# Weights of an encoder step laid out on the host in the order of the kernel's loads

## The chip, the cores and the metric

The kernel runs on one core of a Trainium2 chip. The metric is device time in microseconds (us) of one execution. The engines are PE (TensorE, matmuls), DVE (VectorE), ACT (ScalarE), POOL (GpSimd) and SP (SyncE, which here issues every transfer); 16 DMA engines move data between HBM and the on-chip memory. A float32 product is made of float32r parts: a value is split into a high and a low part, and three matmuls (high x high, high x low, low x high) are added up.

## The reference

One layer of a streaming encoder is computed for 2048 prompt tokens and 32 sample tokens, in blocks of 512, 512, 512 and 544 tokens:

```python
def split_proj(a, w_in):
    z = a @ w_in
    qa, ka, va, qb, kb, vb = jnp.split(
        z, [WIDTH_A, 2 * WIDTH_A, 3 * WIDTH_A, 3 * WIDTH_A + WIDTH_B, 3 * WIDTH_A + 2 * WIDTH_B], axis=-1)
...
def merge(oa, ob, subln_g, out_norm_b, w_out, lam_init):
    oa = rmsnorm(oa, subln_g, SUBLN_EPS) * (1.0 - lam_init)
    ob = rmsnorm(ob.reshape(B, T, WIDTH_B), out_norm_b)
    return jnp.concatenate([oa.reshape(B, T, WIDTH_A), ob], axis=-1) @ w_out
...
def ffn_ple(h, p, g_mlp, w_up, w_down, w_ple_gate, w_ple_proj):
    c = rmsnorm(h, g_mlp)
    h = h + jnp.square(jax.nn.relu(c @ w_up)) @ w_down
    return h + jax.nn.sigmoid(h @ w_ple_gate) * (p @ w_ple_proj)
```

Between split_proj and merge stand a differential attention over all earlier tokens (group A, four heads of two maps) and a band attention over the last 576 tokens (group B, eight heads). The model width is 1024; w_in has 3072 columns, w_up 4096, w_down 4096 rows, w_ple_proj 256 rows.

## The kernel before, in words

The work runs in stages. First the rows of x are normalized and turned (prep), and w_in makes v (vtile, 256 columns at a time) and q and k (proj, 128 columns at a time); attention of groups A and B is woven between. q, k, v, attention outputs (oT) and the residual (hS) go through scratch buffers in HBM, so transfers of weights share the DMA engines with these. From about 800 us follow the output projection (outproj), the MLP and the gate (gate) by token block: blocks 0 and 1 with an ordinary MLP (mlp_up, mlp_down), blocks 2 and 3 from about 2200 us with mlp7, which makes the up-projection out of seven products of half-sized parts in place of eight.

Every weight comes in units of 512 KB: a raw tile "wr" of 4 KB in each of 128 partitions is loaded by SP, then split into high and low parts: ACT writes the high part, POOL (in a few places DVE) the low one. Function wunit does that, for all weights but those of mlp7's up-projection; the tiles are wh and wl, or, late in the kernel, "piece" tiles of half the size, which turn round in rings of buffers. There are two raw buffers, three or four in some stages; SP issues a load once the last reader of its buffer is done. A unit of w_in (q, k), w_up, w_out or w_ple_gate is the 1024 rows of 128 columns, in each partition eight rows of 512 bytes; a unit for v is 512 rows of 256 columns, four pieces of 1 KB; a unit of w_down or w_ple_proj is 256 rows of 512 columns, two pieces of 2 KB.

In mlp7 a chunk of 256 columns of w_up comes as two loads of 512 rows each. Its function weights (L1239 on) makes the parts a11, a21 (first load) and a12, a22 (second load), and with DVE the sums a11 - a21 (L1255), s2 = a22 minus that (L1256), s1 (L1257) and s4 (L1258). The sums overwrite the raw tiles. The first chunk of a block goes into a tile "lead".

The order of the instructions on every engine is made by a scheduler ahead of the run; it simulates the program with its own estimate of each instruction and transfer. Engines work through their rows in order, so a row that waits holds up all rows behind it.

Of the kernel before, what the change touches and what calls it, by code (L numbers as in the profile page):

```python
# [13 lines left out]
F32 = mybir.dt.float32  # L14
# [6 lines left out]
P = 128  # L21
# [122 lines left out]
class Kern:  # L144
# [266 lines left out]
        return [(0, 512 * b, 512), (512, SP + PAST, SS)]  # L411

    def vunits(self, grp, c, **kw):
        col = 1536 * grp + 1024 + 256 * c
        wv = self.a["w_in"][0][:, col : col + 256].rearrange("(k p) c -> p k c", p=P)
        return [self.wunit(wv[:, 4 * i : 4 * i + 4], [4, 256], **kw) for i in range(2)]

    def vtile(self, b, i, grp, c, u, acts, sg, mm):
        nc, a = self.nc, self.a
# [29 lines left out]

    def proj(self, half, grp, acts, sg, mm, tp, vs=range(2), gs=range(4)):  # L450
        nc, a = self.nc, self.a
        W = a["w_in"][0]
        base = 1536 * grp
        ko_p, ko_s = (a["ka_p"], a["ka_s"]) if grp == 0 else (a["kb_p"], a["kb_s"])
        for c in vs:
            u = self.vunits(grp, c)
            for b in half:
                for i in range(len(toks(b))):
                    self.vtile(b, i, grp, c, u, acts, sg, mm)
                    yield  # L460
        late = []
        for g in gs:
            gi = 4 * grp + g
            for kind in range(2):
                col = base + 512 * kind + P * g
                wh, wl = self.wunit(W[:, col : col + P].rearrange("(k p) c -> p k c", p=P), [8, P])
                for b in half:
                    aH, aL = acts[b]
                    hi = sg.tile([P, BLK], F32R, tag="qh", bufs=2, name="qh")
                    lo = sg.tile([P, BLK], F32R, tag="ql", bufs=2, name="ql")  # L470
                    if kind == 1:
                        raw = sg.tile([P, BLK], F32, tag="kr", bufs=2, name="kr")
                    for s0, n in SUBS[b]:
                        ps = mm.tile([P, 512], F32, tag="mm", name="qps")
                        self.mm3(
                            ps[:, :n],
                            [
                                (wh[:, k], wl[:, k], aH[:, k, s0 : s0 + n], aL[:, k, s0 : s0 + n])
                                for k in range(8)
                            ],  # L480
                        )
# [12 lines left out]
                        self.split(h_, l_, r_, "act", "pool")  # L494
                    if kind == 0:
                        for i, t in enumerate((hi, lo)):
                            self.dma(
                                self.qS[gi, :, :, 2 * b : 2 * b + 2, i].rearrange("m r k c -> (m r) k c"),
                                t[:, :512].rearrange("p (k c) -> p k c", c=256),
                            )  # L500
                            if b == 3:
                                self.dma(
                                    self.qS[gi, :, :, 8, i, :SS].rearrange("m r c -> (m r) c"), t[:, 512 : 512 + SS]
                                )
                        yield
                        continue
                    for i, t in enumerate((hi, lo)):
                        for c0, kc, n in self.ktok(b):
                            self.dma(self.kS[gi, i, :, kc : kc + n], t[:, c0 : c0 + n])
                    yield  # L510

                    def knat(b=b, g=g, raw=raw):
                        if grp == 0 or b == 3:
                            tps = tp.tile([P, 4, P], F32, tag="mm", name="ktp")
                            for i in range(4):
                                nc.tensor.transpose(tps[:, i], raw[:, i * P : i * P + P], self.ident)
                            kn = sg.tile([P, 4, P], F32, tag="kn", bufs=2, name="kn")
# [439 lines left out]
    def outproj(self, b, wk, oact, ps, acc):  # L957
        nc, a = self.nc, self.a
        n, t0 = BN[b], 512 * b
        W = a["w_out"][0]  # L960
        sq = wk.tile([P, BLK], F32, tag="acc", bufs=2, name="sqacc2")[:, :n]
        acc.append(sq)
        for d in range(8):
            wh, wl = self.wunit(W[:, P * d : P * d + P].rearrange("(k p) c -> p k c", p=P), [8, P])
# [145 lines left out]

    def mlp_up(self, ch, nf, blocks, st, wk, up, mm):
        nc = self.nc
        Wu = self.a["w_up"][0]
        us, w = {}, {}
        order = [(f, b) for f in range(nf) for b in blocks]
        if ch == 0:
# [1 line left out]
        for f, b in order:  # L1118
            ft = nf * ch + f
            if f not in w:  # L1120
                w[f] = self.wunit(Wu[:, P * ft : P * ft + P].rearrange("(k p) c -> p k c", p=P), [8, P])
            wh, wl = w[f]
            h, cH, cL = st[b]
            uh = up.tile([P, up.aw], F32R, tag="u", name="uh")
# [13 lines left out]

    def mlp_down(self, ch, nf, blocks, us, st, wk, mm):
        nc = self.nc  # L1140
        Wd = self.a["w_down"][0]
        nd = 8 // nf
        for dh in range(nf):
            wh, wl = self.wunit(
                Wd[P * nf * ch : P * nf * (ch + 1), P * nd * dh : P * nd * (dh + 1)].rearrange(
                    "(f p) c -> p f c", p=P
                ),
                [nf, P * nd],
            )
            for d in range(nd):  # L1150
                dd = nd * dh + d
                for b in blocks:
# [36 lines left out]
    def mlp7(self, b, hh, box, ops, wk, up, mm, md):  # L1189
        nc = self.nc  # L1190
        n = BN[b]
        m = n // 2
        Wu, Wd = self.a["w_up"][0], self.a["w_down"][0]

        def downs(ch, us):
            for dh in range(2):
                wh, wl = self.wunit(
                    Wd[2 * P * ch : 2 * P * (ch + 1), 512 * dh : 512 * dh + 512].rearrange("(f p) c -> p f c", p=P),
                    [2, 512],
                )  # L1200
# [38 lines left out]
        def weights(ch, w, piece):  # L1239
            raws = []  # L1240
            for i in range(2):
                raws.append(self.rawp.tile([P, 4, 256], F32, bufs=2, name="wr"))
                self.dma(
                    raws[i],
                    Wu[512 * i : 512 * i + 512, 256 * ch : 256 * ch + 256].rearrange("(k p) c -> p k c", p=P),
                )
            a11, a21 = raws[0][:, :, :P], raws[0][:, :, P:]
            a12, a22 = raws[1][:, :, :P], raws[1][:, :, P:]
            names = ("a11", "a12", "s2", "s1")
            for x in names:  # L1250
                w[x] = piece([4, P])
# [71 lines left out]
    def gate(self, b, h, up, act, md, wk=None, made=None):  # L1323
        nc, a = self.nc, self.a
        n, t0 = BN[b], 512 * b
        Wg, Wp = a["w_ple_gate"][0], a["w_ple_proj"][0]
        pT = [[up.tile([P, BLK], F32R, tag="u", name="pT") for _ in range(2)] for _ in range(2)]
        for i in range(2):
            for k in range(2):
# [13 lines left out]
            for k in range(8):  # L1343
                self.split(hH[k], hL[k], h[:, k, :n], "act", "dve" if k % 2 else "pool")
        for dq in range(2):
            ph, pl = self.wunit(
                Wp[:, 512 * dq : 512 * dq + 512].rearrange("(k p) c -> p k c", p=P), [2, 512]
            )
            for d4 in range(4):
                d = 4 * dq + d4  # L1350
                wh, wl = self.wunit(Wg[:, P * d : P * d + P].rearrange("(k p) c -> p k c", p=P), [8, P])
# [335 lines left out]
}  # L1687


# [26 lines left out]
```

## Time and profile before

| | |
|---|---|
| runs before | 3106.78, 3105.26, 3100.71 us; median 3105.26 us |
| the profiled execution | 3106.68 us, of which 3104.9 us are the span from the first to the last instruction |
| mean granted TensorE clock | 0.988 |
| PE busy | 2990.2 us, 96% of the span |
| DVE, ACT, POOL busy | 59%, 57%, 60% |
| transfers | 523,279 packets, 539.19 MB, 174 GB/s over the span |
| weight loads | 402 of 512 KB: w_up 128, w_down 128, w_in 74, w_out 32, w_ple_gate 32, w_ple_proj 8 |

The profile is of one execution. Its rows of waits name an engine, a tile and a line, what that engine waited for, and then the total in us, how often, and the longest. A row of the timeline has the start, the duration in us and what the instruction does (written tile <- read tiles); in brackets stands the idle time just before and what ended it. The slices are 40 equal parts of the span, each digit the busy share in tenths. A row of stages has the stretch, its length, the busy time and instructions of PE, PE's weight loads, DVE, ACT and POOL, the granted clock, the busy share of the DMA engines and GB/s.

### The profile page before, as it was taken

Reading aid. Unit: us, or ns where it says so; the run is one execution under the profiler, and the core shown is the slowest. Engines: PE = TensorE matmul, PEld = TensorE weight load, DVE = VectorE, ACT = ScalarE, POOL = GpSimd, SP = SyncE. Lnnn points to the kernel's source line nnn. Section 1 sums busy time; section 2 is a strip of 40 time slices with the busy share of each in tenths; the row PEclk is TensorE's granted clock in tenths of the full one; section 3 lists DMA queues with packets and bytes.
Section 4 is the critical chain, followed back from the end, with each engine's and each line's share of the span. In section 5 each row is a group of like instructions: output and inputs, shape, how many; then the busy total and the mean of one; then the engine's idle time right before and its main releaser. Section 6 shows DMA issues by size and latency. Waiting matters only on the chain. (4 is left out here: it accounts for less than half of the span.)

```text
span 3104.9 us, 51763 instructions
## 1 busy us (share of the span) xinstructions
PE 2990.2 (96%) x17801; PEld 2637.0 (85%) x17801; DVE 1826.0 (59%) x4404; ACT 1776.4 (57%) x3434; POOL 1852.7 (60%) x2512
## 2 busy tenths in 40 slices
PE   8999989999899999999999999999899999999998
PEld 7788879899777888878888888878788887999998
DVE  6157565564565455456666656635667885576663
ACT  6256565765666666556556556554655555554545
POOL 2456746413446544556655555677878888767674
PEclk9999999999999999999999999999999999999999
DMA  9798776976877554555655454348434446333231
GB/s 283 258 263 247 224 218 187 280 221 186 247 230 226 159 155 136 154 157 167 196 152 140 124 145 139 123 150 260 155 116 130 146 158 226 118 109 102 90 117 57
DMA packets 523279, 539.19 MB, mean 174 GB/s; under 512 B 38749, under 2 KB 401569, under 8 KB 523017
## 3 DMA queue, kind: packets, MB, share of 16 engines
q1 hardware_dynamic: 523016, 535.89, 57.5%
q8 instruction: 141, 2.31, 0.3%
q14 instruction: 122, 0.99, 0.1%
HBM read 421.97 MB, written 117.75 MB: 174 GB/s over the span
## 5 line engine op out<-in xcount | busy, mean ns | idle before, releaser
L176 POOL TENSOR_TENSOR wl<-wr,wh 128x256 fp32r<-128x256 f32 x648 | 478.9, 771 | 317.8 <-ACT wh L181 277.9
L181 ACT ACTIVATE piece<-wr 128x512 fp32r<-128x512 f32 x406 | 245.4, 624 | 265.0 <-PE ups L217 111.2
L176 POOL TENSOR_TENSOR piece<-wr,piece 128x256 fp32r<-128x256 f32 x404 | 327.5, 836 | 104.6 <-ACT piece L181 85.7
L181 ACT ACTIVATE wh<-wr 128x1024 fp32r<-128x1024 f32 x228 | 240.4, 1055 | 188.1 <-PE ups L217 46.8
L166 POOL TENSOR_TENSOR wl<-wr,wh 128x256 fp32r<-128x256 f32 x264 | 201.9, 797 | 188.1 <-ACT wh L181 185.3
L216 PE MATMUL dps<-uh,piece 128*128 128x272 f32 (+1 forms) x768 | 246.3, 324 | 6.2 <-DVE h L1217 2.5
L166 POOL TENSOR_TENSOR piece<-wr,piece 128x256 fp32r<-128x256 f32 x280 | 235.1, 871 | 26.7 <-ACT piece L181 25.5
L218 PE MATMUL dps<-uh,piece 128*128 128x272 f32 (+1 forms) x768 | 246.9, 324 | 1.8 <-POOL piece L166 1.6
L217 PE MATMUL dps<-ul,piece 128*128 128x272 f32 (+1 forms) x768 | 247.3, 323 | 0.2 <-DVE ul L187 0.2
L216 PE MATMUL ups<-cs,piece 128*128 128x256 f32 (+1 forms) x864 | 245.8, 285 | 0.9 <-DVE r L1228 0.8
L217 PE MATMUL ups<-cs,piece 128*128 128x256 f32 (+1 forms) x864 | 245.7, 285 | 0.0
L218 PE MATMUL ups<-cs,piece 128*128 128x256 f32 (+1 forms) x864 | 245.5, 284 | 0.0
L216 PE MATMUL qps<-aH,wh 128*128 128x512 f32 (+1 forms) x640 | 227.9, 357 | 1.1 <-DVE ql L488 1.1
L217 PE MATMUL qps<-aL,wh 128*128 128x512 f32 (+1 forms) x640 | 228.0, 356 | 0.0
L218 PE MATMUL qps<-aH,wl 128*128 128x512 f32 (+1 forms) x640 | 227.6, 356 | 0.0
L1217 DVE TENSOR_TENSOR h<-h,dps 128x272 f32<-128x272 f32 (+1 forms) x384 | 188.9, 514 | 52.6 <-PE dps L218 51.7
L1169 DVE TENSOR_TENSOR h<-h,dps 128x512 f32<-128x512 f32 x256 | 173.3, 682 | 69.0 <-PE dps L218 67.4
L665 ACT ACTIVATE e<-e,nm 128x128 f32<-128x128 f32 (+16 forms) x136 | 157.2, 1156 | 94.9 <-DVE nm L663 92.9
L216 PE MATMUL dps<-uh,wh 128*128 128x512 f32 x512 | 207.0, 404 | 1.8 <-DVE h L1169 1.8
L216 PE MATMUL ups<-cH,wh 128*128 128x512 f32 x512 | 202.8, 397 | 1.9 <-ACT cH L181 1.9
L217 PE MATMUL ups<-cL,wh 128*128 128x512 f32 x512 | 202.5, 396 | 1.8 <-POOL cL L166 1.2
L218 PE MATMUL ups<-cH,wl 128*128 128x512 f32 x512 | 202.7, 396 | 0.0
(311 smaller groups left out, 9369.8 us busy)
## 6 DMA issues: line engine op xcount, KB each, us to landing
wr<-w_up SPq DMA_DIRECT2D x128, 512.0 KB, 4.0
wr<-w_down SPq DMA_DIRECT2D x128, 512.0 KB, 3.9
wr<-w_in SPq DMA_DIRECT2D x74, 512.0 KB, 5.5
q<-qS SPq DMA_DIRECT2D x128, 256.0 KB, 5.2
v<-vSa SPq DMA_DIRECT2D x64, 512.0 KB, 4.8
ka<-kS SPq DMA_DIRECT2D x32, 512.0 KB, 6.8
wr<-w_out SPq DMA_DIRECT2D x32, 512.0 KB, 4.6
wr<-w_ple_gate SPq DMA_DIRECT2D x32, 512.0 KB, 4.2
```

The costliest lines, as they stand in the source:

```text
L166: nc.gpsimd.tensor_tensor(out[:, sl], a[:, sl], b[:, sl], op=op)
L176: nc.gpsimd.tensor_tensor(out[:, sl], a[:, sl], b[:, sl], op=op)
L181: nc.scalar.activation(hi, raw, AF.Copy)
L216: nc.tensor.matmul(ps, lh, rh, start=start and i == 0, stop=False)
L217: nc.tensor.matmul(ps, lh, rl, start=False, stop=False)
L218: nc.tensor.matmul(ps, ll, rh, start=False, stop=stop and i == n - 1)
L665: nc.scalar.activation(row, row, AF.Exp, bias=nmx, accum_out=z[:nr, m : m + 1])
L1169: nc.vector.tensor_tensor(hv, hv, ps, op=ALU.add)
L1217: nc.vector.tensor_tensor(hv, hv, ps, op=ALU.add)
```

## The change

On the host, numpy cuts each weight into the units of the loads and lays them one behind the other, so that a unit is 128 rows (partitions) of 4 KB without a gap. w_in becomes two arrays, w_qk and w_v. The function tiled does it, and each load names its unit by a number:

```diff
+def tiled(w, k, c):
+    r = w.shape[0] // (k * P)
+    w = w.reshape(r, k, P, -1, c).transpose(0, 3, 2, 1, 4)
+    return np.ascontiguousarray(w.reshape(-1, P, k, c))
...
+    w_in = arrays.pop("w_in")[0]
+    arrays["w_qk"] = tiled(np.concatenate([w_in[:, :1024], w_in[:, 1536:2560]], 1), 8, P)
+    arrays["w_v"] = tiled(np.concatenate([w_in[:, 1024:1536], w_in[:, 2560:]], 1), 4, 256)
+    for n, k, c in (("w_out", 8, P), ("w_up", 8, P), ("w_down", 2, 512), ("w_ple_gate", 8, P), ("w_ple_proj", 2, 512)):
+        arrays[n] = tiled(arrays[n][0], k, c)
...
-                wh, wl = self.wunit(W[:, col : col + P].rearrange("(k p) c -> p k c", p=P), [8, P])
+                wh, wl = self.wunit(a["w_qk"][8 * grp + 4 * kind + g], [8, P])
...
             raws = []
             for i in range(2):
-                raws.append(self.rawp.tile([P, 4, 256], F32, bufs=2, name="wr"))
-                self.dma(
-                    raws[i],
-                    Wu[512 * i : 512 * i + 512, 256 * ch : 256 * ch + 256].rearrange("(k p) c -> p k c", p=P),
-                )
-            a11, a21 = raws[0][:, :, :P], raws[0][:, :, P:]
-            a12, a22 = raws[1][:, :, :P], raws[1][:, :, P:]
+                raws.append(self.rawp.tile([P, 8, P], F32, bufs=2, name="wr"))
+                self.dma(raws[i], self.a["w_up"][2 * ch + i])
+            a11, a12 = raws[0][:, :4], raws[0][:, 4:]
+            a21, a22 = raws[1][:, :4], raws[1][:, 4:]
```

The other loads are changed like the one of proj. The tiles, their buffers and the splits stay. In mlp7 a load is now all 1024 rows of 128 columns (the unit that mlp_up uses), so the first load holds a11 and a12 and the second a21 and a22.

The scheduler's order is the same on PE, DVE, ACT and POOL up to the gate of block 0, which is woven with the first chunk of mlp7 for block 2. (Line numbers after the change are lower: L1234 to L1237 are the sums that were L1255 to L1258, L1011 was L1017, L1338 to L1343 were L1362 to L1367.) ACT at this gate, before: piece_25153 is the high part of the second half of a gate weight (raw tile wr_25146), cs the parts of the MLP's input made from tmp, sig the gate's activation.

```order
L181 ACTIVATE cs_24507<-tmp_24983 128x256
L1364 ACTIVATE sig_25041<-sig_25041 128x512
L181 ACTIVATE cs_24505<-tmp_24980 128x256
L181 ACTIVATE cs_24499<-tmp_25057 128x256
L181 ACTIVATE cs_24503<-tmp_24980 128x256
L181 ACTIVATE piece_25153<-wr_25146 128x512
L181 ACTIVATE cs_24501<-tmp_25060 128x256
```

ACT at the same place after the change:

```order
L1340 ACTIVATE sig_25041<-sig_25041 128x512
L181 ACTIVATE cs_24507<-tmp_24983 128x256
L181 ACTIVATE cs_24499<-tmp_25057 128x256
L181 ACTIVATE cs_24505<-tmp_24980 128x256
L181 ACTIVATE piece_25153<-wr_25146 128x512
L181 ACTIVATE cs_24501<-tmp_25060 128x256
L181 ACTIVATE cs_24509<-tmp_25060 128x256
L1343 ACTIVATE sig_25041<-sig_25041 128x512
L181 ACTIVATE cs_24503<-tmp_24980 128x256
```

The row cs_24503 has moved from ahead of piece_25153 to behind it. DVE at the same gate, before, from the first sum of mlp7's first chunk on (wr_25200 and wr_25202 are its two raw tiles):

```order
L1255 TENSOR_TENSOR wr_25200<-wr_25200 128x4x128
L1256 TENSOR_TENSOR s2_25210<-wr_25202,wr_25200 128x512
L1366 TENSOR_SCALAR sig_24964<-gps_24939,sig_24964 128x512
L1017 TENSOR_SCALAR tmp_24980<-tmp_24980,g_mlp_s_245,r_24417 128x512
L1257 TENSOR_TENSOR wr_25200<-s2_25210,wr_25200 128x4x128
L187 TENSOR_TENSOR lead_25199<-s2_25210,lead_25199 128x512
L1017 TENSOR_SCALAR tmp_24983<-tmp_24983,g_mlp_s_245,r_24417 128x512
L1381 TENSOR_TENSOR sig_24964<-sig_24964,pps_24970 128x512
L1258 TENSOR_TENSOR wr_25202<-wr_25202,s2_25210 128x4x128
```

DVE there after the change:

```order
L1234 TENSOR_TENSOR wr_25202<-wr_25200,wr_25202 128x512
L1342 TENSOR_SCALAR sig_24964<-gps_24939,sig_24964 128x512
L1011 TENSOR_SCALAR tmp_24980<-tmp_24980,g_mlp_s_245,r_24417 128x512
L1235 TENSOR_TENSOR s2_25210<-wr_25202 128x512
L1011 TENSOR_SCALAR tmp_24983<-tmp_24983,g_mlp_s_245,r_24417 128x512
L1357 TENSOR_TENSOR sig_24964<-sig_24964,pps_24970 128x512
L1236 TENSOR_TENSOR wr_25200<-s2_25210,wr_25200 128x512
L1237 TENSOR_TENSOR wr_25200<-wr_25200,s2_25210 128x512
L187 TENSOR_TENSOR lead_25199<-s2_25210,lead_25199 128x512
```

The first sum reads both raw tiles, and the second only the second one; the second sum has moved behind two rows of the gate and the norm. In the later chunks of mlp7, here in block 3, DVE had before (r0, u2, u3 and r1 are the results of the seven products, h the residual that dps is added to):

```order
L1228 TENSOR_TENSOR u2_30228<-t1_30199,ups_30229 128x272
L1255 TENSOR_TENSOR wr_30624<-wr_30624 128x4x128
L1228 TENSOR_TENSOR u3_30258<-u2_30228,ups_30259 128x272
L1228 TENSOR_TENSOR r0_30197<-u2_30228,ups_30275 128x272
L187 TENSOR_TENSOR piece_30345<-wr_30314,piece_30344 128x512
L1228 TENSOR_TENSOR r1_30198<-u3_30258,ups_30293 128x272
L187 TENSOR_TENSOR ul_30194<-r0_30197,uh_30193 128x544
L1228 TENSOR_TENSOR r0_30357<-t1_30359,ups_30374 128x272
L1228 TENSOR_TENSOR u2_30388<-t1_30359,ups_30389 128x272
L1256 TENSOR_TENSOR s2_30642<-wr_30626,wr_30624 128x512
L1217 TENSOR_TENSOR h_30191<-h_30191,dps_30415 128x272
```

DVE in the same chunk after the change:

```order
L187 TENSOR_TENSOR ul_30194<-r0_30197,uh_30193 128x544
L1210 TENSOR_TENSOR r0_30357<-t1_30359,ups_30374 128x272
L1210 TENSOR_TENSOR u2_30388<-t1_30359,ups_30389 128x272
L1234 TENSOR_TENSOR wr_30626<-wr_30624,wr_30626 128x512
L1235 TENSOR_TENSOR s2_30642<-wr_30626 128x512
L1199 TENSOR_TENSOR h_30191<-h_30191,dps_30415 128x272
```

The first sum has moved down seven rows, to stand just ahead of the second.

More of the change, by code (lines that the diff above doesn't have):

```diff
@@ L413, in vunits @@
     def vunits(self, grp, c, **kw):
-        col = 1536 * grp + 1024 + 256 * c
-        wv = self.a["w_in"][0][:, col : col + 256].rearrange("(k p) c -> p k c", p=P)
-        return [self.wunit(wv[:, 4 * i : 4 * i + 4], [4, 256], **kw) for i in range(2)]
+        return [self.wunit(self.a["w_v"][4 * i + 2 * grp + c], [4, 256], **kw) for i in range(2)]
     def vtile(self, b, i, grp, c, u, acts, sg, mm):
@@ L451, in proj @@
         nc, a = self.nc, self.a
-        W = a["w_in"][0]
-        base = 1536 * grp
         ko_p, ko_s = (a["ka_p"], a["ka_s"]) if grp == 0 else (a["kb_p"], a["kb_s"])
@@ L464, in proj @@
             for kind in range(2):
-                col = base + 512 * kind + P * g
-                wh, wl = self.wunit(W[:, col : col + P].rearrange("(k p) c -> p k c", p=P), [8, P])
+                wh, wl = self.wunit(a["w_qk"][8 * grp + 4 * kind + g], [8, P])
                 for b in half:
@@ L959, in outproj @@
         n, t0 = BN[b], 512 * b
-        W = a["w_out"][0]
         sq = wk.tile([P, BLK], F32, tag="acc", bufs=2, name="sqacc2")[:, :n]
@@ L963, in outproj @@
         for d in range(8):
-            wh, wl = self.wunit(W[:, P * d : P * d + P].rearrange("(k p) c -> p k c", p=P), [8, P])
+            wh, wl = self.wunit(a["w_out"][d], [8, P])
             h = wk.tile([P, BLK], F32, tag="tmp", bufs=self.nt, name="hd")[:, :n]
@@ L1112, in mlp_up @@
         nc = self.nc
-        Wu = self.a["w_up"][0]
         us, w = {}, {}
@@ L1120, in mlp_up @@
             if f not in w:
-                w[f] = self.wunit(Wu[:, P * ft : P * ft + P].rearrange("(k p) c -> p k c", p=P), [8, P])
+                w[f] = self.wunit(self.a["w_up"][ft], [8, P])
             wh, wl = w[f]
@@ L1140, in mlp_down @@
         nc = self.nc
-        Wd = self.a["w_down"][0]
         nd = 8 // nf
         for dh in range(nf):
[L1144 to L1148, printed above, removed]
-            )
+            wh, wl = self.wunit(self.a["w_down"][nf * ch + dh], [nf, P * nd])
             for d in range(nd):
@@ L1192, in mlp7 @@
         m = n // 2
-        Wu, Wd = self.a["w_up"][0], self.a["w_down"][0]
         def downs(ch, us):
             for dh in range(2):
[L1197 to L1200, printed above, removed]
+                wh, wl = self.wunit(self.a["w_down"][2 * ch + dh], [2, 512])
                 for d in range(4):
@@ L1241, in weights @@
             for i in range(2):
-                raws.append(self.rawp.tile([P, 4, 256], F32, bufs=2, name="wr"))
-                self.dma(
-                    raws[i],
-                    Wu[512 * i : 512 * i + 512, 256 * ch : 256 * ch + 256].rearrange("(k p) c -> p k c", p=P),
-                )
-            a11, a21 = raws[0][:, :, :P], raws[0][:, :, P:]
-            a12, a22 = raws[1][:, :, :P], raws[1][:, :, P:]
+                raws.append(self.rawp.tile([P, 8, P], F32, bufs=2, name="wr"))
+                self.dma(raws[i], self.a["w_up"][2 * ch + i])
+            a11, a12 = raws[0][:, :4], raws[0][:, 4:]
+            a21, a22 = raws[1][:, :4], raws[1][:, 4:]
             names = ("a11", "a12", "s2", "s1")
@@ L1325, in gate @@
         n, t0 = BN[b], 512 * b
-        Wg, Wp = a["w_ple_gate"][0], a["w_ple_proj"][0]
         pT = [[up.tile([P, BLK], F32R, tag="u", name="pT") for _ in range(2)] for _ in range(2)]
@@ L1345, in gate @@
         for dq in range(2):
-            ph, pl = self.wunit(
-                Wp[:, 512 * dq : 512 * dq + 512].rearrange("(k p) c -> p k c", p=P), [2, 512]
-            )
+            ph, pl = self.wunit(a["w_ple_proj"][dq], [2, 512])
             for d4 in range(4):
                 d = 4 * dq + d4
-                wh, wl = self.wunit(Wg[:, P * d : P * d + P].rearrange("(k p) c -> p k c", p=P), [8, P])
+                wh, wl = self.wunit(a["w_ple_gate"][d], [8, P])
                 for s0, sn in SUBS[b]:
```

## The prediction

> **What bounds the kernel now.** I read the page from the top (span, busy times, slices), then the waits of the tensor engine, and behind its longest ones the waits of the engine that it waits for, in the same 20 us.
>
> ```profile
> span 3104.9 us, 51763 instructions
> PE 2990.2 (96%) x17801; PEld 2637.0 (85%) x17801; DVE 1826.0 (59%) x4404; ACT 1776.4 (57%) x3434; POOL 1852.7 (60%) x2512
> DMA  9798776976877554555655454348434446333231
> core 0: 3104.9 us, clock 0.988
> ```
>
> PE is the bound: it is idle for 3104.9 - 2990.2 = 114.7 us in all, and its mean granted clock of 0.988 costs about 0.012 x 3105 = 37 us more. No change to weight loads can bring more than these together. The DMA row says where loads are scarce: the first ten slices (0 to 780 us) are 60 to 90% busy, the last five 10 to 30%. What ends the idle time of PE, in the whole run:
>
> ```profile
> PE css L1096 <- ACT sh L181: 5.9, 1, 5.9
> PE gps L216 <- ACT piece L181: 5.2, 2, 5.0
> PE xp L380 <- DMA x<-x_prompt: 4.4, 1, 4.4
> PE vps L216 <- ACT wh L181: 3.3, 2, 2.5
> PE sb L831 <- DMA q<-qS: 2.5, 1, 2.5
> PE dps L216 <- ACT piece L181: 2.3, 6, 0.8
> PE o L723 <- DMA v<-vSa: 2.3, 2, 1.9
> PE s L650 <- DVE e L657: 4.9, 1, 4.9
> PE sb L831 <- DVE stb L834: 3.4, 1, 3.4
> PE ups L216 <- ACT cH L181: 1.9, 2, 1.1
> ```
>
> (Columns: total us, times, longest. The last three rows are those of 380 to 400, 660 to 680 and 960 to 1000 us.) Few wait for a weight by name: vps, gps and dps, 10.8 us. But behind the others, in the same 20 us, stands an engine held by a transfer, and it is rarely a weight:
>
> ```profile
> DVE vhl L183 <- DMA vSb<-vhl: 5.5, 1, 5.5
> DVE vhl L183 <- DMA vSa<-vhl: 6.0, 1, 6.0
> DVE tmp L998 <- DMA tmp<-hS: 14.8, 5, 5.6
> ACT oraw L932 <- DMA oraw<-oT: 7.3, 1, 7.3
> ```
>
> These are VectorE at 380, 660 and 960 us and ScalarE at 1300 us, just before the stalls of s, sb, ups and css above. So transfers reach PE where the DMA engines are crowded, through instructions queued behind a late one.
>
> **The change, step by step. (1) Packets.** The loads stay 402 of 512 KB each, so the bytes do not change. By the shapes in the order of SP, 178 are cut in 512-byte pieces (1024 packets), 88 in 1 KB (512) and 136 in 2 KB (256); afterwards each has 128 of 4 KB. That removes 178 x 896 + 88 x 384 + 136 x 128 = 210,688 packets of
>
> ```profile
> q1 hardware_dynamic: 523016, 535.89, 57.5%
> ```
>
> What is a packet worth? The fastest landing of each kind, where the queue was empty, tells it best; first w_up (512 bytes) and w_down (2 KB) between 1000 and 1500 us, then x (4 KB rows) in the whole run:
>
> ```profile
> DMA to landing us min/median/max: 3.9/4.1/10.0
> DMA to landing us min/median/max: 3.5/4.2/11.5
> DMA to landing us min/median/max: 3.5/7.0/8.7
> ```
>
> Each of 16 engines moves 64 packets of the first and 16 of the second: 0.4 us for 48 packets, 8.3 ns each. The third shows a floor: from 2 KB to 4 KB nothing more is seen. The other end comes from two stages, 100 to 500 and 2700 to 3000 us:
>
> ```profile
> q1 hardware_dynamic: 95091, 94.14, 78.8%
> q1 hardware_dynamic: 21705, 29.87, 30.9%
> ```
>
> Their engine time is 0.788 x 16 x 400 = 5043 and 0.309 x 16 x 300 = 1483 us. Solved for a price per packet and one per byte that is 13.8 ns and 0.040 ns. I take 8.3 ns, measured on single loads, and keep 0 and 13.8. A 512-byte load then lands 56 x 8.3 ns = 0.47 us sooner (0 to 0.77), a 1 KB load 0.2, a 2 KB load 0 to 0.1.
>
> The row on landing is also where the Trainium skill speaks against this change: "DMA: Bandwidth & Descriptors", Specifications, gives 512 B as the smallest transfer at line rate, by which cutting fewer pieces brings nothing; the 0.4 us between 3.9 and 3.5 disagree mildly. The same page of the Trainium skill, Why small descriptors are slow, counts about 3 cycles for each packet beside one for each 32 bytes, 19 against 16 for 512 B; by that (an estimate from the page) the service of a load, 524,288 bytes x 0.040 ns over 16 engines = 1.3 us, would shrink by some 14%, 0.2 us, and the terms (2) and (3) would halve.
>
> **(2) Crowded stage.** Up to 1000 us there are 70 loads of 512-byte and 24 of 1 KB pieces, which free 70 x 0.47 + 24 x 0.2 = 38 us on every DMA engine; with the slices at some 75 to 80%, that is 5% of its busy time. A late transfer there has one or two weight loads ahead of it, so it comes about 0.4 us sooner. About ten stalls of PE end with a late transfer (of the rows above css, q, v, s, sb and ups, 20.9 us, and a few small ones like them): -4 us, between 0 and -10. The first x, 4.4 us, is loaded ahead of every weight and stays.
>
> **(3) Direct waits for weights.** vps twice 0.2, the one long gps wait in (4), about two other waits for 512-byte weights 0.4 each: -1.2 us (0 to -2). SP issues a load faster, but nothing waits for SP alone:
>
> ```profile
> L157 SPq DMA_DIRECT2D x<-x_prompt x16: 333/460/4044, 0.7 to 417.3; - x16
> L157 SPq DMA_DIRECT2D wr<-w_in x74: 368/386/1839, 1.7 to 782.1; - x74
> ```
>
> The shortest issue is 35 ns apart; at nothing, and 402 x 35 ns = 14 us of SP if it ever were the bound.
>
> **(4) What the scheduler moves.** Until the gate of block 0 all compute engines keep their order. There the rows of ScalarE shown above put the split of the second half of a gate weight (piece_25153) ahead of cs_24503. In the trace this is PE's longest weight wait:
>
> ```profile
> 2220.69 0.42 ACT L181 ACTIVATE cs<-tmp 128x256 fp32r<-128x256 f32 x1 [1.31 <-DVE tmp L1031]
> 2221.01 0.61 ACT L181 ACTIVATE piece<-wr 128x512 fp32r<-128x512 f32 x1
> 2221.68 0.79 PE L216 MATMUL gps<-hu,piece 128*128 128x512 f32 x1 [4.98 <-ACT piece L181]
> 2222.27 0.63 PE L217 MATMUL gps<-hu,piece 128*128 128x512 f32 x1
> 2226.95 0.39 PE L216 MATMUL pps<-pT,piece 128*128 128x512 f32 x1
> ```
>
> The split stands behind a cs that waits 1.31 us for VectorE. Without that cs it starts 1.31 + 0.3 = 1.6 us sooner: -1.6 us. If what is now ahead of it is no later, that is; VectorE's first difference waits for both loads now, and a late one would take back up to the same 1.6. After the stall the matmuls last 0.63 us up to 2226.95 and 0.39 from there: twelve of this half, 0.24 us each, so a stall short enough to keep the clock could bring 2.9 us more. SP keeps its order but for three loads in the last third. In the second chunk of blocks 2 and 3 the first w_up load goes behind the 2 MB load of h and the chunk's second w_up load, which went behind h already; the sum needed that one too, so the last of the two lands at most one load, 1.3 us, later, twice. I put it at nothing, since the additions into h wait for the 2 MB as well. PE itself moves rows in 27 places, the largest being the two column sums (css) of block 3, some 80 rows later; their result is read only in the stage after, so I put that at nothing, and at 5.9 us, the one css wait above, if a reader stood there.
>
> **(5) The sums of the 7-product MLP.** L1255 now needs both w_up loads of a chunk, where it needed the first, and L1256 none:
>
> ```profile
> L1256 DVE TENSOR_TENSOR s<-wr 128x512 f32<-128x512 f32 x32 | 28.8, 900 | 41.6 <-DMA wr<-w_up 41.4
> L1255 DVE TENSOR_TENSOR wr<-wr 128x512 f32<-128x512 f32 x32 | 28.5, 891 | 29.7 <-DMA wr<-w_up 27.4 <-POOL piece L176 1.4 <-POOL piece L166 0.8
> 2900.00:3000.00 100.00, 100.00 (x801) 100.00 (x801) 62.44 (x127) 48.68 (x85) 70.20 (x91) 1.00 0.30 96
> ```
>
> So VectorE no longer does L1255 while the second load flies: up to 32 x 0.89 = 28.5 us later in sum, with the additions into h, the relu inputs and piece splits queued behind it, for which PE waits. The scheduler answers by putting L1255 just ahead of L1256, so the new wait stands where the old one stood. In the last row PE has no idle time while VectorE has 38%: covered, at 0. Without that cover it is +28.5.
>
> **Sum.** The profiled execution took 3106.68 us (span 3104.9 and 1.8 around it), 1.4 above the median of 3105.26. Idle time removed: 4 + 1.2 + 1.6 = 6.8 us. The clock loses 37 us for 114.7 of idle time, 0.32 for each; I add 0.32 x 6.8 = 2.2. 3106.7 - 9.0 = **3097.7 us**, own range 3092 to 3102.
>
> **The rivals.** *Nothing from packets*: 512-byte pieces already run at full rate, or the hardware cuts 4 KB again; the medians of w_up and w_down, 4.1 and 4.2 us, speak for it, the minima against. Then only (4) is left, 1.6 x 1.32 = 2.1: 3104.6. The Trainium skill's line-rate sentence stands with this one. *More than that*: at 13.8 ns (2) is -7 and (3) -2, and the stall of (4) gets short enough to keep the clock, -1.6 and -2.9; with 0.32 x 9 = 2.9 on the first two, 3106.7 - 16.4 = 3090.3. For it speaks that three of the first ten slices stand at 90% or more. *Slower*: the wait of (5) reaches PE. Place: the 32 chunks of blocks 2 and 3 between 2200 and 3000 us; it decides once VectorE comes later to an addition into h than PE's free PSUM tiles last. Half of the chunks give +14.2 against -5.2 of (2) and (3): 3115.7. Against it stands the last row above.
>
> **How the numbers follow.** Forecast 0.42, nothing 0.29, more 0.15, slower 0.14. The bound of 0.2% is 6.2 us, about what a measurement of this kernel tells from no change: faster is below 3099.0, slower above 3111.5. Some 0.30 of the forecast and all of "more" are faster, 0.45; 0.12 and "nothing" are the same, 0.41; slower 0.14. The range reaches to 3088 at "more" and to 3111 short of "slower", and leaves out about two in ten.
>
> **What would show it.** Right: queue 1 has about 312,000 packets and 535.9 MB; its share falls from 57.5% to 54% (13,168 packets an engine x 8.3 ns = 109 us); the fastest w_up lands in 3.5 us; PE's idle time near 108 us, less of it before 1000 us; the gps wait near 3.4 us. Wrong: the share stays (packets cost nothing), or PE waits for h or r of VectorE after 2200 us.

## The result, and the profile after

The changed kernel took **3088.38 us** (median of 3084.97, 3087.03, 3088.62, 3092.94 and 3088.38), against 3105.26 before: 16.9 us less, a ratio of 0.9951 (15.2 us) with a 95% interval of 0.9937 to 0.9966. The forecast was 3097.7, faster. The sign is right, but the gain is twice the forecast one. The time lies below the sum's own range (3092 to 3102) and only 0.4 us inside the wider one, which reaches to 3088 for the rival "more than that" (3090.3). Why it comes near that rival's number is another matter than the rival said.

The page of the changed kernel, its profiled execution being the one of 3084.97 us:

```profile
span 3083.2 us, 51724 instructions
PE 2980.3 (97%) x17801; PEld 2632.2 (85%) x17801; DVE 1827.9 (59%) x4404; ACT 1774.8 (58%) x3434; POOL 1849.7 (60%) x2512
DMA  8788776966877454645655444357433446333231
core 0: 3083.2 us, clock 0.990
q1 hardware_dynamic: 312328, 535.89, 55.3%
```

The reader is to see three things. The packets are the 312 thousand of step (1), with the same bytes. PE is idle for 3083.2 - 2980.3 = 102.9 us where it was 114.7: -11.8. And PE's busy time, for the same 17,801 matmuls, is 9.9 us shorter. The mean granted clock accounts for about half of that (it lost 0.0117 x 3104.9 = 36.2 us before and 0.0102 x 3083.2 = 31.5 after); where the rest comes from is not shown. Together that is 21.7 us between these two executions, 4.8 more than between the medians, so a single trace is good for a few microseconds only.

What ends PE's idle time after the change (total us, times, longest):

```profile
PE sb L826 <- DVE stb L829: 11.2, 12, 2.9
...
PE gps L216 <- ACT piece L181: 6.9, 1, 6.9
PE s L645 <- DVE e L652: 6.1, 3, 4.5
PE css L1090 <- ACT sh L181: 5.9, 1, 5.9
PE xp L380 <- DMA x<-x_prompt: 4.5, 1, 4.5
PE dps L216 <- ACT piece L181: 4.4, 7, 1.3
...
PE sb L826 <- DMA q<-qS: 2.6, 1, 2.6
PE vps L216 <- ACT wh L181: 2.6, 1, 2.6
PE ups L216 <- ACT cH L181: 2.3, 2, 1.6
...
PE o L718 <- DMA v<-vSa: 0.4, 1, 0.4
```

The large stalls that I had counted on are mostly still there: css 5.9 (was 5.9), q 2.6 (2.5), the long one of s 4.5 (4.9), ups 2.3 (1.9), the long one of sb 2.9 (3.4); only v has nearly gone, 0.4 (2.3). The gate's wait for a weight, gps, has grown from 5.0 to 6.9. The landings of w_up (first row) and w_down between 1000 and 1500 us:

```profile
DMA to landing us min/median/max: 3.3/3.5/9.8
DMA to landing us min/median/max: 3.4/4.0/11.0
```

SP's issue of the q and k weights (count: shortest/median/longest ns):

```profile
L157 SPq DMA_DIRECT2D wr<-w_qk x50: 327/352/866, 9.9 to 767.4; - x50
```

w_up lands 0.6 us sooner (3.9/4.1 before), w_down 0.1 to 0.2, and an issue takes 327 ns at the least (368 before). The shorter issue goes with the pieces, as the sooner landing does, and no run here tells the two apart; it is 0.04 us beside 0.6. Last, the groups of VectorE's sums in the 7-product MLP, and after them the stretch in which I saw them covered:

```profile
L1234 DVE TENSOR_TENSOR wr<-wr 128x512 f32<-128x512 f32 x32 | 31.0, 969 | 44.9 <-DMA wr<-w_up 44.5
L1235 DVE TENSOR_TENSOR s<-wr 128x512 f32<-128x512 f32 x32 | 29.3, 915 | 0.4
```

```profile
2900.00:3000.00 100.00, 100.00 (x801) 100.00 (x801) 61.06 (x126) 50.14 (x87) 72.15 (x94) 1.00 0.35 117
```

The wait of L1234 is now 44.5 us in place of 27.4 + 41.4 on two lines, and in this row PE still has no idle time.

### The profile page after: what moved, and what is told of

Same layout as the page of the kernel before. It is cut to its first block, busy times and chain, and to the rows that moved or that the text cites. A ratio compares the mean times of both kernels' runs of the same rounds, so it can differ in the third digit from the quotient of the medians.

```text
span 3083.2 us, 51724 instructions
## 1 busy us (share of the span) xinstructions
PE 2980.3 (97%) x17801; PEld 2632.2 (85%) x17801; DVE 1827.9 (59%) x4404; ACT 1774.8 (58%) x3434; POOL 1849.7 (60%) x2512
## 2 busy tenths in 40 slices
DMA packets 312590, 539.19 MB, mean 175 GB/s; under 512 B 38748, under 2 KB 174240, under 8 KB 312328
## 3 DMA queue, kind: packets, MB, share of 16 engines
q1 hardware_dynamic: 312328, 535.89, 55.3%
## 4 chain that ended last, share of the span: by engine, by line
PE 57%; DVE 3%; DMA 3%; POOL 2%; ACT 1%; issue 1%; SPq 0%; DVEq 0%; POOLq 0%; ACTq 0%
PE dps L216 7%; PE dps L218 7%; PE dps L217 7%; PE ups L218 6%; PE ups L216 6%; PE ups L217 6%; PE s L645 3%; PE gps L216 2%; PE gps L217 2%; PE gps L218 2%; PE tpp L704 1%; PE ob L878 1%; PE tpb L848 1%; PE o L719 1%; PE o L720 1%
```

## Experiments

The first guess from the two traces was the theory **crowd**: at the same instructions the changed kernel was already 14.8 us ahead at 500 us, so the gain seemed to be made in the q, k and v projections. Its rivals: **in proportion** (a removed packet is worth the same wherever it is), **addresses** (what helps is that the pieces of a load now lie side by side), **order** (the moved instructions). In every kernel below but the one without w_in and the changed kernel itself, the engines run in the order of the kernel before, row for row.

### Only w_in, and all but w_in

The first kernel has of the change only this, and w_v likewise; the second undoes just this in the changed kernel.

```diff
-                wh, wl = self.wunit(W[:, col : col + P].rearrange("(k p) c -> p k c", p=P), [8, P])
+                wh, wl = self.wunit(a["w_qk"][8 * grp + 4 * kind + g], [8, P])
```

> The kernel before, with only w_in laid out in 4 KB pieces (the q, k and v weights); the order of every engine is that of the kernel before. The change as a whole took 3105.3 to 3088.4 us, -16.9. Theory 'crowd' (the gain is made where the DMA engines are crowded, in the q, k and v projections, because shorter loads there let every transfer behind them land sooner): about 3092 us, -11 to -15, with PE's idle time before 500 us near 25 us in place of 33. Theory 'in proportion' (each removed packet is worth the same wherever it is): w_in has 50 x 896 + 24 x 384 = 54,016 of 210,688 removed packets, 26%, so -4.3, 3101 us. Theory 'order' (the moved instructions bring the gain): 3105 us.

> The changed kernel, with w_in alone left in its old layout; the order of every engine is that of the changed kernel. Theory 'crowd': 3101 us, -2 to -6, with PE's idle time before 500 us as in the kernel before, 33 us. Theory 'in proportion': 74% of the gain, 3092.8 us. Theory 'order': 3088 us.

Measured: only w_in 3098.75 us beside 3104.39, ratio 0.9983 (0.9973 to 0.9994), -5.3 us. All but w_in 3094.13, ratio 0.9971 (0.9960 to 0.9982), -9.0. PE's idle time up to the instruction at which the 14.8 us were read is 28.8 us with only w_in and 31.2 with all but w_in, beside 33.1 before and 25.0 after. "Crowd" wanted -11 to -15 and -2 to -6 and falls by the first (interval -8.4 to -1.9); the second (-12.4 to -5.6) just touches it. "In proportion" wanted -4.3 and about -12, "order" nothing and the whole gain. Part of the 14.8 us was luck of the traced execution of before: the kernel with near addresses, next, has the same packets and order and is 4.8 us quicker at the same place.

### Near addresses with the old pieces; far addresses with 4 KB

Near addresses, against the change in the order of before (below):

```diff
-    w = w.reshape(r, k, P, -1, c).transpose(0, 3, 2, 1, 4)
-    return np.ascontiguousarray(w.reshape(-1, P, k, c))
+    w = w.reshape(r, k, P, -1, c).transpose(0, 3, 1, 2, 4)
+    return np.ascontiguousarray(w.reshape(-1, k, P, c))
...
-                wh, wl = self.wunit(a["w_out"][d], [8, P])
+                wh, wl = self.wunit(a["w_out"][d].rearrange("k p c -> p k c"), [8, P])
```

Far addresses: all units of an array stored with the partition first (the pieces of a load are then 8 to 128 KB apart, by the number of an array's units, not 40 to 256 as the expectation has it):

```diff
-    return np.ascontiguousarray(w.reshape(-1, P, k, c))
+    return np.ascontiguousarray(w.reshape(-1, P, k, c).transpose(1, 0, 2, 3))
...
-                wh, wl = self.wunit(a["w_out"][d], [8, P])
+                wh, wl = self.wunit(a["w_out"][:, d], [8, P])
```

> Every load's 512 KB stand together in memory, as in the changed kernel, but in the pieces of the kernel before (512 bytes, 1 KB, 2 KB), so packets and orders are those of before and only the addresses differ. Theory 'crowd' and every theory on packets: 3105 us within 4, 523,016 packets, fastest w_up landing 3.9 us as before. Theory 'addresses' (what helps is that the pieces of a load lie side by side in memory, not that they are fewer): 3088 us, fastest w_up landing near 3.5 us with all 523,016 packets.

> The counterpart of the run with near addresses: 4 KB pieces, 312,328 packets, orders of before, but the 128 pieces of one load lie far apart in memory (every weight array is stored with the partition first, so that the pieces of one load are 40 to 256 KB apart). So far: near addresses with the old pieces -2.5 (interval -5.9 to 0.6), 4 KB pieces with near addresses -18.3. 'Packets': it keeps the gain, -16 to -18, 3087. 'Addresses': what the near addresses bring is lost; -0 to -3 if they are all of it, -13 to -15 if they are the 2.5 that the first run hints at.

Measured: near addresses in old pieces 3099.79 us beside 3104.39, ratio 0.9992 (0.9981 to 1.0002), -2.5. Far addresses in 4 KB pieces 3090.62 beside 3102.96, ratio 0.9954 (0.9940 to 0.9968), -14.3. So the piece size carries the gain; whether addresses add some 2 to 4 us these intervals do not settle. The landing of w_up between 1000 and 1500 us with near addresses and old pieces:

```profile
DMA to landing us min/median/max: 3.8/4.0/9.7
```

With far addresses and 4 KB pieces:

```profile
DMA to landing us min/median/max: 3.4/3.6/7.6
```

The fastest landing goes with the pieces (512 bytes 3.8, 4 KB 3.4) and hardly with the addresses.

### The change in the order of before

```diff
-                raws.append(self.rawp.tile([P, 8, P], F32, bufs=2, name="wr"))
-                self.dma(raws[i], self.a["w_up"][2 * ch + i])
-            a11, a12 = raws[0][:, :4], raws[0][:, 4:]
-            a21, a22 = raws[1][:, :4], raws[1][:, 4:]
+                raws.append(self.rawp.tile([P, 4, 256], F32, bufs=2, name="wr"))
+                self.dma(raws[i], self.a["w_up7"][16 * i + ch])
+            a11, a21 = raws[0][:, :, :P], raws[0][:, :, P:]
+            a12, a22 = raws[1][:, :, :P], raws[1][:, :, P:]
...
+    arrays["w_up7"] = tiled(arrays["w_up"][0], 4, 256)
```

> The changed kernel, except that the 7-product MLP's w_up loads hold the same quarters as in the kernel before (still in 4 KB pieces, from an array of their own); the compute engines then have the order of the kernel before to the last row. Theory 'crowd': the order is worth little, 3088 us within 3; the longest gate wait back near 5.0 us where it was 6.9, so perhaps 1 to 3 us less. My prediction's term for the moved instructions (-2.1) would make it 3090.5. Theory 'order': 3105 us.

> The changed kernel itself again, on the chip of the runs beside it, as their yardstick: 3088 us within 3. The same change in the order of before took 3084.9 us (-18.3); if the moved instructions cost nothing it comes out the same, if they cost what the longer gate stall and the dps waits suggest, 2 to 4 us more.

Measured: 3084.94 us beside 3104.39, ratio 0.9941 (0.9929 to 0.9953), -18.3. The changed kernel, run again: 3086.71 beside 3104.49, ratio 0.9945 (0.9929 to 0.9961), -17.1. "Order" falls: without the moved instructions the whole gain is there. This is the fastest version run, but by 1 to 3 us, which the intervals do not separate from the change as it is.

My term (4) is not borne out either. The gate's stall in the order of before, here 7.6 us long:

```profile
2199.44 0.42 ACT L181 ACTIVATE cs<-tmp 128x256 fp32r<-128x256 f32 x1 [1.41 <-DVE tmp L1023]
2200.31 0.42 ACT L181 ACTIVATE cs<-tmp 128x256 fp32r<-128x256 f32 x1
2201.44 0.42 ACT L181 ACTIVATE cs<-tmp 128x256 fp32r<-128x256 f32 x1 [0.72 <-DVE tmp L1011]
2203.17 0.42 ACT L181 ACTIVATE cs<-tmp 128x256 fp32r<-128x256 f32 x1 [1.31 <-DVE tmp L1025]
2203.49 0.61 ACT L181 ACTIVATE piece<-wr 128x512 fp32r<-128x512 f32 x1
2204.16 0.79 PE L216 MATMUL gps<-hu,piece 128*128 128x512 f32 x1 [7.61 <-ACT piece L181]
```

And in the changed kernel:

```profile
2196.05 0.42 ACT L181 ACTIVATE cs<-tmp 128x256 fp32r<-128x256 f32 x1 [2.06 <-DVE tmp L1023]
2197.18 0.42 ACT L181 ACTIVATE cs<-tmp 128x256 fp32r<-128x256 f32 x1 [0.72 <-DVE tmp L1011]
2198.04 0.42 ACT L181 ACTIVATE cs<-tmp 128x256 fp32r<-128x256 f32 x1 [0.45 <-DVE tmp L1024]
2198.37 0.61 ACT L181 ACTIVATE piece<-wr 128x512 fp32r<-128x512 f32 x1
2199.03 0.79 PE L216 MATMUL gps<-hu,piece 128*128 128x512 f32 x1 [6.93 <-ACT piece L181]
```

The cs with the 1.31 us wait is indeed no longer ahead of the split. But all cs but one there wait for a tmp of VectorE, so ScalarE moves at VectorE's pace, and an earlier one now waits 2.06 us in place of 1.41. Between these two traces the new order is worth 0.7 us, not 1.6. Both stalls are longer than the 4.98 of before, while a wait of 1.6 us for a split on GpSimd, which came 9 us ahead of the stall in the kernel before, is gone in both. The longer stall does not need the change: with only w_in laid out, where this gate's weights and the order are those of before, it is 7.6 us too. In the order of before it is 4.9 to 5.1 us in three traces and 6.5 to 7.6 in six, and in the changed order 6.9 to 7.0 in three. What decides between the two lengths stays open.

### Early weights, late weights

Three kernels, each the one before with some weights laid out: w_in and w_out (half of w_out's 32 loads come before 1000 us, half at 2000 to 2200); w_up, w_down, w_ple_gate and w_ple_proj; and of these only the 7-product MLP's and w_ple, with arrays of their own:

```diff
-                wh, wl = self.wunit(
-                    Wd[2 * P * ch : 2 * P * (ch + 1), 512 * dh : 512 * dh + 512].rearrange("(f p) c -> p f c", p=P),
-                    [2, 512],
-                )
+                wh, wl = self.wunit(self.a["w_down7"][2 * ch + dh], [2, 512])
...
-                self.dma(
-                    raws[i],
-                    Wu[512 * i : 512 * i + 512, 256 * ch : 256 * ch + 256].rearrange("(k p) c -> p k c", p=P),
-                )
+                self.dma(raws[i], self.a["w_up7"][16 * i + ch])
```

> The kernel before, with w_in and w_out laid out in 4 KB pieces: all the weights that are loaded up to about 1000 us, where the DMA engines are 60 to 90% busy, and nothing later but w_out of the later blocks. Orders as before. So far: the whole change -16.9, w_in alone -5.3 (interval 1.9 to 8.4), all but w_in -9.0, the whole change in the order of before -18.3. 'Crowd' (the gain is made in the crowded stage; then w_out must carry what w_in alone did not): -12 to -14, 3091. 'In proportion' (each removed packet is worth 17 us / 210,688 = 0.08 us per 1000, wherever it is): 82,688 packets, -6.6, 3098.

> The complement: w_up, w_down, w_ple_gate and w_ple_proj laid out in 4 KB pieces, w_in and w_out as before, orders as before. 'Crowd': -2 to -5, 3101. 'In proportion': 128,000 packets, -10.3, 3094. With the run of w_in and w_out it must add up to about -18 if the two parts don't touch each other.

> The kernel before with only the weights loaded after about 2150 us laid out in 4 KB pieces: those of the 7-product MLP (w_up, w_down), w_ple_gate and w_ple_proj; orders of before; 62,464 packets fewer. There the DMA engines are 30 to 40% busy. 'In proportion' (17 us / 210,688 each): -5.0, 3099.5. 'Direct waits' (after 2150 us, kernels with these weights in 4 KB pieces were on average about 6 us quicker than those without, in single traces, and VectorE's waits for w_up in 2300 to 2790 us fell from 39.4 to 26.1 us): -4 to -6. 'Crowd', and my prediction, which put these waits at nothing because TensorE had no idle time in 2900 to 3000 us: -0 to -1.5, 3103.5.

Measured: w_in and w_out 3093.54 us beside 3104.49, ratio 0.9969 (0.9957 to 0.9981), -9.6. The complement 3091.31, ratio 0.9963 (0.9949 to 0.9976), -11.5 (-15.8 to -7.5): that alone refutes "crowd" (-2 to -5). The two parts add up to -21.1, beside -18.3 for the whole, which the intervals allow. The last stage by itself 3098.10 beside 3102.96, ratio 0.9986 (0.9973 to 0.9998), -4.3, where I had put about nothing; its interval, -8.4 to -0.6, still reaches down to what "crowd" allows (0 to -1.5), so it takes the lengths of the stages below to tell them apart. The waits within 2300 to 2790 us show part of where it comes from: VectorE's for w_up, and below the dots PE's for splits of ScalarE, h and r. In the kernel before:

```profile
DVE s L1256 <- DMA wr<-w_up: 19.1, 13, 3.1
DVE wr L1255 <- DMA wr<-w_up: 14.3, 11, 3.0
...
PE dps L216 <- DVE h L1217: 2.5, 2, 1.8
PE dps L216 <- ACT piece L181: 2.3, 6, 0.8
```

In the near-address kernel (old pieces, order of before):

```profile
DVE s L1235 <- DMA wr<-w_up: 21.3, 15, 3.3
DVE wr L1234 <- DMA wr<-w_up: 18.1, 14, 3.2
...
PE dps L216 <- ACT piece L181: 2.6, 6, 0.8
PE ups L216 <- DVE h L1199: 1.6, 1, 1.6
PE dps L216 <- DVE h L1199: 1.6, 2, 1.4
```

The change in the order of before:

```profile
DVE s L1235 <- DMA wr<-w_up: 13.4, 11, 2.3
DVE wr L1234 <- DMA wr<-w_up: 12.7, 11, 2.5
...
PE dps L216 <- ACT piece L181: 1.7, 4, 0.8
PE ups L216 <- DVE r L1210: 0.7, 1, 0.7
```

The change as it is:

```profile
DVE wr L1234 <- DMA wr<-w_up: 18.0, 12, 2.8
...
PE dps L216 <- ACT piece L181: 4.4, 7, 1.3
PE ups L216 <- DVE r L1210: 1.6, 1, 1.6
PE dps L216 <- DVE r L1210: 0.4, 1, 0.4
```

With sooner weights VectorE waits 26.1 us in place of 33.4 and 39.4. A kernel that is ahead has part of the stage outside this window: a wait of PE for h, 1.3 us, stands at 2298 us in the 4 KB kernel with the order of before and at 2294 in the changed one, and so in no row above. Over the whole of the last stage (from 2150.4 us in the kernel before) VectorE waits 66 to 72 us for w_up with old pieces, 54 to 56 with 4 KB in the order of before and 40 to 45 in the changed order; PE waits 1.1 to 3.2 us for h with old pieces and 1.3 in each kernel with 4 KB; its idle time is 20.3 to 21.1 us with old pieces and 17.1 to 20.5 with 4 KB in the order of before. In the changed order VectorE waits least, yet PE is idle for 20.7 to 22.2 us: it waits more for splits of ScalarE and, in two of three traces, for r.

### All in 512 bytes

The change in the order of before, with each unit stored as eight pieces of 128 x 128, and loaded so (pieces of w_v, w_up7, w_down and w_ple_proj are cut smaller than ever):

```diff
...
+            raw = raw.rearrange("p k (t c) -> p k t c", c=P)
+            src = src.rearrange("(k t) p c -> p k t c", k=k)
```

> Every weight load in 512-byte pieces, those of w_v and of the 7-product MLP's w_up (1 KB before) and of w_down and w_ple_proj (2 KB before) too; each load's pieces lie together in memory; orders as before. That makes 672,520 packets, 149,504 more than before. 'In proportion': +12, 3116. 'Crowd': most of the added packets come after 1000 us, where there is room; +2, 3106. A floor near 512 bytes (the line rate of the Trainium skill, 'DMA: Bandwidth & Descriptors', Specifications, by which 512-byte pieces cost nothing more than larger ones): 3104.

Measured: 3109.12 us beside 3104.49, ratio 1.0018 (1.0009 to 1.0028), +5.6 (+2.8 to +8.7). There is no floor at 512 bytes, and "crowd" (+2) is too low; "in proportion" gave +12, which is outside the interval on the other side, though beside the near-address kernel, whose addresses it shares, the distance is 5.6 + 2.5 = 8.1. Its queue 1:

```profile
q1 hardware_dynamic: 672520, 535.89, 59.3%
```

Its w_down between 1000 and 1500 us, now in 512-byte pieces:

```profile
DMA to landing us min/median/max: 3.8/4.4/10.6
```

w_down's fastest landing goes from 3.5 us (2 KB) to 3.8 (512 bytes).

### Together

| weights in 4 KB pieces | packets | us against before |
|---|---|---|
| none, all in 512 bytes, near | 672,520 | +5.6 |
| none, near | 523,016 | -2.5 |
| w_in | 469,000 | -5.3 |
| last stage | 460,552 | -4.3 |
| w_in, w_out | 440,328 | -9.6 |
| all but w_in, w_out | 395,016 | -11.5 |
| all but w_in, changed order | 366,344 | -9.0 |
| all, far | 312,328 | -14.3 |
| all, changed order (two series) | 312,328 | -15.2, -17.1 |
| all | 312,328 | -18.3 |

(us: ratio less 1, times 3104.4.) A straight line through these and the kernel before, 523,016 at 0, has 0.063 us for 1000 packets and misses no run by more than 3.2 us, within the reach of the intervals (3 to 5 us each way). Of the theories "in proportion" fits best, across early and late weights, but a strict proportion is not shown. Counted from the kernel before, removed packets bring 0.087 us for 1000 (18.3 for 210,688; interval 0.069 to 0.104) and added ones cost 0.037 (5.6 for 149,504; 0.019 to 0.058). Counted from the near-address kernel it is 0.075 and 0.054, which the intervals allow to be the same. So either addresses bring some 2 us of the gain, or a packet is worth less where pieces get smaller; the runs leave this open.

The traces say the same by stages. Four instructions of ScalarE, the same in every trace, cut the run; in the kernel before they start at 498.6, 997.4, 2150.4 and 3090.1 us. Mean length of each stage over the profiled executions, by whether its weights (those named; the second also has 21 loads of w_in, the third 16 of w_out) are in old or 4 KB pieces. The kernel in 512 bytes is left out; in its one trace the stages last 492.3, 499.5, 1154.1 and 951.6 us, so it is slow in the last two, which have nearly all of its added packets.

| stage, weights | old pieces | 4 KB, order of before | 4 KB, changed order |
|---|---|---|---|
| to 498.6, w_in | 494.8 (5 traces) | 488.7 (6, both) | |
| to 997.4, w_out | 499.1 (5) | 495.0 (6, both) | |
| to 2150.4, w_up, w_down | 1149.8 (5) | 1145.9 (6, both) | |
| to 3090.1, 7-product MLP, gate | 941.4 (4) | 936.2 (4) | 940.6 (3) |

Each stage gains 4 to 6 us in the mean; in the first three the single lengths still overlap by 1 to 2 us. In the last one the 4 KB kernels with the order of before (935.0 to 937.8) lie apart both from the old pieces (939.7 to 943.1) and from the changed order (939.3 to 941.3). So the changed order gives back some 4 us there. Only traces show that; the times of whole runs do not separate the two.

## Why the prediction was right in sign and half in size

**(1) Packets.** 312,328, as worked out. The landing was priced well: w_up 0.47 us sooner was forecast, 0.6 came (0.5 in the order of before). A packet was priced at 8.3 ns of an engine, by which the share of queue 1 was to fall to 54%; it fell to 55.3%. DMA time (share times span) went from 0.575 x 3104.9 = 1785 to 0.553 x 3083.2 = 1705 us, 80 us for 13,168 packets, 6.1 ns each; by the second trace of the changed kernel (0.561 x 3080.6 = 1728) it is 4.3 ns. From the near-address kernel to the one in 512 bytes it is 43 us for 9,344, 4.6 ns. So the price in engine time is lower, 4 to 6 ns, for pieces made larger and made smaller. And this engine time does not by itself set the gain: in their one trace the far 4 KB pieces used 0.571 x 3089.3 = 1764 us, only 21 less than before, and still they gained 14.3. The Trainium skill's "DMA: Bandwidth & Descriptors", Specifications, has line rate from 512 B; the fastest landings, 3.8 us at 512 bytes and 3.4 at 4 KB, disagree. The extra cycles for each packet, of which that page of the Trainium skill speaks in Why small descriptors are slow, agree in kind.

**(2) Crowded stage.** Forecast -4, own bounds 0 to -10; w_in and w_out together brought -9.6 (-5.9 to -13.3). The first two stages together take 989.8 to 997.4 us in the four traces with w_in and w_out in old pieces and 980.6 to 986.8 in the five with both in 4 KB, 9.7 less in the mean. The step that failed is "about ten stalls of PE end with a late transfer", each 0.4 us shorter, as the whole of the gain: css, q, s and ups stood at 15.2 us in all and stand at 15.3, and with v and the long sb the six went from 20.9 to 18.6. What went is mostly in smaller waits: up to the end of the second stage, waits of 2 us and more make 24.0 us before and 25.0 after, shorter ones 35.5 and 26.6. The first 1000 us of the kernel before:

```profile
0.00:1000.00 1000.00, 937.86 (x5751) 828.36 (x5752) 538.00 (x1689) 592.24 (x1300) 479.56 (x719) 0.98 0.80 237
```

And of the changed one:

```profile
0.00:1000.00 1000.00, 946.28 (x5829) 837.38 (x5830) 542.96 (x1710) 604.79 (x1324) 491.08 (x736) 0.99 0.78 241
```

8.4 us less idle time (62.1 to 53.7) at a slightly higher clock. This pair is on the high side: over the four and the five traces idle time in these two stages is 58.4 and 52.8 us in the mean. That fewer packets cause it is shown; by which chain each small wait shrinks is not, and stays open.

**(3) Direct waits.** Forecast -1.2, counted from waits in which PE names a weight. vps (3.3 to 2.6) fits its own part, though it is 2.8 in the near-address kernel with the old pieces. But the weights from w_up on, of which (2) counted only the first few, brought -11.5 (-7.5 to -15.8). What was missed is that sooner weights pay in stages with free DMA engines too. In the last stage VectorE's shorter waits for w_up go with it; through which rows PE gains in the ordinary MLP, 1149.8 to 1145.9 us, is not shown.

**(4) The gate's stall.** Forecast -1.6, to a stall of 3.4 us. It failed: the stall is 6.9 to 7.0 us in the three traces with the changed order. Taking one cs away from ahead of the split helps little when VectorE's tmp sets the pace, and in the order of before the stall's length varies by 2.7 us without that row having moved.

**(5) The sums.** Put at 0 because PE had no idle time in the quoted hundred microseconds. That stretch was not the whole stage: between 2300 and 2790 us PE does wait, the sooner weights are worth 4 to 5 us in the last stage, and the changed order takes about as much back. So 0 came out right by luck, as a sum of two terms that I had both missed. The rival "slower" had a real core of some 4 us where it priced 14.2, but by another path: its sign, waits of PE for h and r, stands at 3.3 us in the last stage before and 3.3 after, while the waits for ScalarE's splits grew.

**The clock.** I added 0.32 us of busy time for each us of idle time, the mean. The two traces have 9.9 for 11.8; over twelve profiled executions busy time falls by 0.65 us for each us of idle time, with much scatter (correlation 0.69). Between the two traces the miss of 12.7 us (21.7 for 9.0) is 5.0 of idle time (11.8 for 6.8) and 7.7 of busy time (9.9 for 2.2); 4.8 of it is these two executions and not their medians.

The rival "more" gave almost the measured time with 13.8 ns a packet and a gate stall short enough to keep the clock. Neither happened: a packet took 4 to 6 ns of an engine, and the stall got longer. Its number is right by accident.

## What to carry to other kernels

Cutting a load into fewer, larger pieces paid here roughly by the number of packets removed, some 0.06 to 0.09 us of run time for 1000, and not by how crowded the DMA engines were. A wait counts even if another engine has it: look through the helper engines that prepare a weight before putting a landing at nothing, and over the whole stage, not a stretch of it. A layout that also re-pairs data can move the scheduler's order; undo that part alone to see what it costs.

## What the runs showed of the hardware

The granted clock falls in a step and not in proportion to idle time. In the kernel before, PE waits 3.4 us until 326.7 us; the granted clock is 1.00 from 319.0 to 325.7 us, 0.50 from there to 332.5, and 1.00 again to 339.0. Over twelve profiled executions, the matmuls in the 8 us after each idle time of PE (up to the next one of 0.5 us or more) are set against the median duration of their shape: after 0.5 to 1.5 us of idle time they last 0.3 us longer in sum (425 cases), after 1.5 to 2 us 0.8 (82), after 2 to 5 us 1.9 (109), after more than 5 us 2.2 (26). They last over 1 us longer in 5% of the first group, in 34%, in 81% and in all of the last. So a wait under 1.5 us cost little clock here, and one over 2 us mostly a whole step.

4 KB pieces that lie far apart kept the DMA engines busy for 1764 us, adjacent ones for 0.561 x 3081.8 = 1729, with the same fastest landing of 3.4 us. With the old pieces it is the other way, 1785 far (the kernel before) and 0.582 x 3097.1 = 1802 near, each from one trace, so a cost of scattered pieces in general is not shown.
